# The value projection of a hybrid attention layer: from four pairs with transposes to one seven-product matrix product with tokens on the partitions

## The chip, the cores and the metric

The kernel runs on one core of one Trainium2 chip. The metric is device time in microseconds (us) of that core, the median of several executions of the same program. The profile that is read here is one more execution, taken with the hardware profiler.

## What is computed

One layer of a hybrid encoder: 1024 tokens, model width 1024, 8 heads of chunked softmax attention (A) and 8 heads of stick-breaking attention (B), then gates, an output projection, a LayerNorm, a SwiGLU feed-forward part and a second LayerNorm. What the change touches is the combined input projection:

```python
h = x @ w_in[l]
qa, ka, va, qb, kb, vb, ga, gb = jnp.split(h, split_pts, axis=-1)
```

Each of qa, ka, va, qb, kb, vb is 1024 tokens by 512 columns (8 heads of 64), all in float32. The attention of a head later multiplies its weights (keys by queries) with its 64 columns of va or vb, and there the tokens (keys) have to lie on the partitions.

## The kernel before, in words

**Precision.** Every float32 operand is split into a high part that the tensor engine takes exactly (fp32r) and a low part, `split` (L109): ScalarE copies the high part, VectorE subtracts it (L110, L111). A product of two operands is three matmuls: high by high, high by low, low by high.

**Pairs by seven products.** The projection works on pairs of 128-column tiles, "left" and "right". A pair with the two halves of the tokens is a two by two block product, done with seven products in place of eight, in the order 1, 2, 6, 5, 7, 3, 4 (`pair_steps`, L185, `product`, L168). Each product is 4 steps over the contraction, 3 matmuls each, so 12 matmuls of 128x128 stationary weights with 512 tokens moving; a pair has 84. The sums of x that these products need are made once at the start (`s_sums`, L300, `s13_split`, L311), those of the weights for each pair (`prep_left`, L129; `right_sums_b`, L146; `right_sums_a`, L157; `prep_last`, L162). Products share three PSUM banks, sx, sy and sz; after a product ScalarE copies a bank into the result tile `c` (L199, L208, L212, L420) or VectorE adds it there (L195).

**The list of work** (L232 to L240) has 17 pairs: a query with its key tile (kind qk, 8 of them), two value tiles (kind v, 4 of them), five pairs of gate tiles (kind g). The order is qk, qk, v, qk, qk, v, ... then the gates. The first (qk) is done plainly, in 96 matmuls (`project_plain`, L338). The names in the profile carry the number in this list: wlp5h is the high part of the left weights of pair 5, wap and wbp are right sums, wc the right column of product 3. Pairs 2, 5, 8 and 11 are values.

**The value pair.** Results come out with columns on the partitions. So `out_v` (L393) transposes each of the two tiles in 8 tensor-engine transposes of 128x128 (L401, tile `vtp`), splits them in 8 pieces of 128x256 and stores two heads of 512 KB with rows of 4 KB (L408, `v_dr`). In attention `load_v` (L572) reads one head of 512 KB back in rows of 4 KB (L576).

**What sets the order.** `run_pairs` (L433) calls the products of a pair one after the other and, between them, the loads and sums of later pairs: after the first product the right weights of the next pair, after the second the left weights of the pair after that. Buffers have tags with a fixed number of slots (L44): `gt` (3) and `kp` (4) for raw weights and their sums, `op` (8) for split weights, the tags qs, kh, kl, v with two slots each (`QKV`, taken in turn) for results. A buffer is handed out when its former content has been read for the last time. The framework schedules: each engine's order is fixed at compile time from a model of when operands and slots are ready, with the order of the code as priority, so that an instruction that is ready can be put ahead of one that comes earlier in the code. At run time each engine, and SP's queue which issues all DMAs, goes strictly in the order so fixed. At the start the first two products of three pairs are put ahead (`first=3`), and `rest_of_start` (L541) then makes what the later products lack.

Of the kernel before, what the change touches and what calls it, by code (L numbers as in the profile page):

```python
# [11 lines left out]
F32 = mybir.dt.float32  # L12
F32R = mybir.dt.float32r
AF = mybir.ActivationFunctionType
ALU = mybir.AluOpType
# [3 lines left out]
P = 128  # L19
# [3 lines left out]
DH = 64  # L23
# [7 lines left out]
HW = 512  # L31
LO, HI = slice(0, HW), slice(HW, 2 * HW)
# [13 lines left out]


@with_exitstack
def hybrid_trunk_kernel(ctx: ExitStack, tc, x, xt, w_first, w_in, b_gate, rel_bias, w_proj,
                        w_out, ln1_g, ln1_b, w_ffn_in, w_ffn_out, ln2_g, ln2_b, out):  # L50


# [3 lines left out]
    nc = tc.nc  # L56
# [3 lines left out]
    dr = ctx.enter_context(tc.tile_pool(name="dr", bufs=1, space=DRAM))  # L60
# [3 lines left out]
    def slot(tag, name, dtype=F32):  # L64
        return pool.tile([P, 1024], dtype, tag=tag, name=name, bufs=SLOTS[tag])
# [15 lines left out]

    mm = nc.tensor.matmul
    tr = nc.tensor.transpose
    dma = nc.sync.dma_start


    ident = cst.tile([P, P], F32, name="ident")
# [5 lines left out]

    q_dr = [dr.tile([2 * P, S], F32, name=f"q_dr{i}") for i in range(8)]
    k_dr = [dr.tile([2 * P, S], F32, name=f"k_dr{i}") for i in range(8)]
    v_dr = dram("v_dr", 16)
    y_dr = dram("y_dr", 8)
    g_dr = dram("g_dr", 16)
    m_dr = dram("m_dr", 8)
# [9 lines left out]
    def split(dst_h, dst_l, src):  # L109
        return (nc.scalar.copy(dst_h, src),  # L110
                nc.vector.tensor_tensor(dst_l, src, dst_h.bitcast(F32), ALU.subtract))  # L111
# [45 lines left out]
    def right_sums_a(W, nm, tag):  # L157
        R, ta = W["R"], W["ta"]
        nc.vector.tensor_tensor(ta[:, HI], R[:, HI], R[:, LO], ALU.subtract)
        W["ha"] = split_w(ta, f"wa{nm}", tag)  # L160
# [71 lines left out]
    work = []  # L232
    for br in range(2):
        for i in range(4):
            work.append(("qk", br * 4 + i, br * 12 + i, br * 12 + 4 + i))
            if i % 2:
                work.append(("v", br * 4 + i - 1, br * 12 + 8 + i - 1, br * 12 + 8 + i))

    N_GATE, N_SQUASHED = 5, 4
    work += [("g", j, 24 + j, 32 + j) for j in range(N_GATE)]  # L240
    Wa = [dict() for _ in work]
# [4 lines left out]
    def right(i):  # L246
        prep_right(Wa[i], f"p{i}", w_in[work[i][3]], "op")
        prep_last(Wa[i], f"p{i}", "kp")
# [123 lines left out]
    def project(i):  # L372
        kind, pair = work[i][:2]
        tl = {}

        def tile_of(side):
            if side not in tl:
                tl[side] = cycle(("qs", "kl") if i < 3 and side == "1" else QKV, f"c{side}_{i}")
            return tl[side]

        def c(name):
            return tile_of(name[1])[:, (LO, HI)[int(name[0]) - 1]]

        def out_qk(side):
            scale = (-0.125 if pair < 4 else 0.125) if side == "1" else 1.0
            t = tl[side]
            h = cycle(QKV, f"hi{side}_{i}", F32R)
            nc.scalar.activation(h, t, AF.Copy, scale=scale)
            nc.vector.scalar_tensor_tensor(t, t, scale, h.bitcast(F32), ALU.mult, ALU.subtract)
            d = (q_dr, k_dr)[side == "2"]  # L390
            store_hl(d[pair], h, t)

        def out_v(side):  # L393
            pr = pair + int(side) - 1
            vs = [cycle(QKV, f"v{pr}_{h}", F32R).rearrange("p (t c) -> p t c", t=8)
                  for h in range(2)]
            for hf in range(2):
                tp = bank("tr", f"vtp{pr}_{hf}")
                for j in range(4):
                    o = hf * HW + j * P  # L400
                    tr(tp[:, j * P:(j + 1) * P], tl[side][:, o:o + P], ident)  # L401
                t3 = tp.rearrange("p (t c) -> p t c", t=4)
                ts_ = slice(4 * hf, 4 * hf + 4)
                for h in range(2):
                    split(vs[h][:, ts_, 0:DH], vs[h][:, ts_, DH:P],
                          t3[:, :, h * DH:(h + 1) * DH])
            for h in range(2):
                dma(v_dr[2 * pr + h].rearrange("p (t c) -> p t c", t=8), vs[h].bitcast(F32))  # L408

        def out_g(side):  # L410
            col = (int(side) - 1) * 8 + pair
            if pair < N_SQUASHED:
                nc.scalar.activation(tl[side], tl[side], AF.Sigmoid, bias=bg[:, col:col + 1])
            dma(g_dr[2 * pair + int(side) - 1], tl[side])

        out = dict(qk=out_qk, v=out_v, g=out_g)[kind]

        def done(name, acc):
            if name == "21":
                nc.scalar.copy(c("21"), acc)  # L420
                out("1")
            elif name == "12":
                out("2")

        return pair_steps(f"p{i}", Wa[i], ops_x, c, done, "pv" if i == 3 else "mm")

    def aside_work(i):
        if i == 2:
            small_inputs()
        if i >= len(work) - 9:  # L430
            store_proj(i - len(work) + 9)

    def run_pairs(steps, left, right, also=lambda i: None, first=2, aside=lambda i: None,  # L433
                  then=lambda: None):

        n = len(steps)
        for j in range(first):
            steps[j][0]()
            steps[j][1]()
        then()  # L440
        for i in range(n):
            rest = steps[i][2:] if i < first else steps[i]
            for j, p in enumerate(rest):
                p()
                if j == 0 and i + 1 < n:
                    right(i + 1)
                if j == 1 and i + 2 < n:
                    left(i + 2)
                aside(i)
            also(i)  # L450
# [88 lines left out]
    s_sums(3)  # L539

    def rest_of_start():  # L541
        for kt in range(4):
            s13_split(kt, LO, HI)
        right_sums_a(Wa[1], "p1", "op")
        for kt in range(4):
            s13_split(kt, HI, LO)
        prep_last(Wa[1], "p1", "kp")

    run_pairs([project(i) for i in range(1, len(work))],
              lambda i: left(i + 1) if i > 2 else left_again(3) if i == 2 else None,  # L550
              lambda i: right(i + 1), first=3, then=rest_of_start, also=aside_work)
    first_gate = 2 * N_GATE
    first_w = begin_gate(first_gate, nc.vector)()

# [17 lines left out]
    def load_v(hd):  # L572

        n = 2 * hd["i"] + hd["h"]
        t = slot("v", f"v{n}", F32R)
        dma(t.bitcast(F32), v_dr[n])  # L576
        hd["v"] = t.rearrange("p (t c) -> p t c", t=8)

    def scores(name, hd, b, c0, n):
        q = hd["qs"][:, b * P:(b + 1) * P]  # L580
# [351 lines left out]
    for n, c in enumerate((6, 7, 5, 4, 0, 1, 2, 3)):  # L932
        if n % 2 == 0:
            w = next_w
# [10 lines left out]
        for hf, cs in enumerate((LO, HI)):  # L945
            acc = bank("sc", f"yBps{c}_{hf}")
# [189 lines left out]
    for half_k in range(2):  # L1136
# [136 lines left out]
    first = load_plain(0, 2, ("bw", "bw", "kp", "kp", "bw", "bw", "bw", "kp"))  # L1273
# [34 lines left out]
def layout(inputs):  # L1308

    arr = {n: np.asarray(a)[0] for n, a in inputs.items()}  # L1310
    x = arr["x"][::-1]
    w_in = granules(arr["w_in"])
    w_first = np.stack([w_in[n].reshape(P, 4, 2 * P) for n in (0, 4)], axis=2)
    x_halves = x.T.reshape(KT, P, 2, HW).transpose(2, 0, 1, 3)
    arrs = dict(
        x=x, xt=x_halves,
        w_first=w_first.transpose(1, 0, 2, 3).reshape(4, P, HW), w_in=w_in, b_gate=arr["b_gate"].reshape(16, P).T,
        rel_bias=arr["rel_bias"],
        w_proj=granules(np.concatenate([arr["w_proj_a"], arr["w_proj_b"]])),
        w_out=arr["w_out"], ln1_g=arr["ln1_g"], ln1_b=arr["ln1_b"],  # L1320
        w_ffn_in=granules(arr["w_ffn_in"]), w_ffn_out=arr["w_ffn_out"],
        ln2_g=arr["ln2_g"], ln2_b=arr["ln2_b"])
    return {n: np.ascontiguousarray(a) for n, a in arrs.items()}
# [14 lines left out]
```

## Time and profile before

| | us |
|---|---|
| median of 3 executions | 1439.76 (1439.72 to 1440.11) |
| the profiled execution, its own time | 1440.54 |
| its span in the profile | 1438.8 |
| TensorE busy | 1425.8 |
| VectorE busy | 1030.5 |
| ScalarE busy | 679.0 |
| GpSimd busy | 267.9 |
| the 64 transposes of values, first and last start | 77.7, 249.0 |

The span leaves out what lies around the program's first and last instruction, 1.7 us here. A busy time counts an instruction from its start to its modelled end; matmuls overlap, so their durations add up to more than the time in which they follow one another. The pitch, from one start to the next, has to be taken from windows or from start times. PE is the tensor engine's matmuls and PEld its loads of stationary operands; ACT is ScalarE, DVE VectorE, POOL GpSimd, and SPq the queue of the engine that issues DMAs. In rows of operations the line is that of the code, L180 being the matmul in `product`.

### The profile page before, as it was taken

How to read it: one execution, taken by the hardware profiler on the slowest of the kernel's cores; microseconds unless marked ns; L12 is line 12 of the kernel's file. 1: busy time of each engine (PE TensorE's matmuls, PEld its weight loads, DVE VectorE, ACT ScalarE, POOL GpSimd, SP SyncE). 2: the span in 40 equal slices, each digit the busy share in tenths (PEclk: the TensorE clock that was granted, in tenths of full speed). 3: DMA queues.
4: the chain of work that ended last, by engine and by line, in shares of the span. 5: the costliest groups of instructions: out<-in, count | busy, mean ns of one | idle time of the engine just before them, and what ended most of it. 6: DMA issues, size and time to landing. Idle time of an engine off the chain costs nothing.

```text
span 1438.8 us, 19267 instructions
## 1 busy us (share of the span) xinstructions
PE 1425.8 (99%) x6760; PEld 1182.0 (82%) x6760; DVE 1030.5 (72%) x1664; ACT 679.0 (47%) x1193; POOL 267.9 (19%) x317
## 2 busy tenths in 40 slices
PE   9999999999999999999999999999999999999997
PEld 7788888888888888888888888888888888888886
DVE  8875665544777878877858957667676755978757
ACT  6444444544888788774312734444444433221201
POOL 0000000001555878850014000000000000100016
PEclk9999999999999999999999999999999999999999
DMA  7555657749777487958512223444444457786602
GB/s 249 154 184 176 173 173 224 279 179 248 203 217 198 146 246 249 269 186 287 167 45 88 69 93 132 146 143 151 161 161 150 153 195 263 289 310 234 205 15 103
DMA packets 87921, 262.95 MB, mean 183 GB/s; under 512 B 11008, under 2 KB 11008, under 8 KB 87824
## 3 DMA queue, kind: packets, MB, share of 16 engines
q1 hardware_dynamic: 87824, 261.72, 55.7%
q8 instruction: 53, 0.87, 0.3%
q14 instruction: 44, 0.36, 0.1%
HBM read 169.89 MB, written 88.11 MB: 179 GB/s over the span
## 4 chain that ended last, share of the span: by engine, by line
PE 90%; DVE 4%; ACT 2%; DMA 1%; issue 1%; SPq 1%; POOL 1%; POOLq 0%; DVEq 0%; ACTq 0%
PE sxf L180 16%; PE sxp L180 10%; PE szf L180 8%; PE dx L1264 6%; PE szp L180 5%; PE gps L495 4%; PE syf L180 4%; PE dz L1264 3%; PE yAps L784 3%; PE syp L180 2%; PE tp_b L695 2%; PE tp_a L695 2%; PE ops L117 2%; PE ops L118 2%; PE ops L120 2%; PE dy L1264 2%
## 5 line engine op out<-in xcount | busy, mean ns | idle before, releaser
L1220 POOL TENSOR_TENSOR wdyt<-wdyt 128x512 f32<-128x512 f32 x8 | 11.2, 1394 | 512.3 <-ACT h L1092 422.6
L672 POOL TENSOR_TENSOR w_b<-w_b,kp_b 128x511 f32<-128x511 f32 (+3 forms) x96 | 96.1, 1013 | 33.1 <-DVE kp_b L667 24.0
L667 DVE TENSOR_TENSOR_SCAN kp_b<-kp_b,ident_ps 128x512 f32<-128x512 f32 (+2 forms) x64 | 56.6, 885 | 23.3 <-ACT kp_b L664 22.5
L664 ACT ACTIVATE kp_b<-sc_b 128x512 f32<-128x512 f32 (+3 forms) x96 | 48.4, 504 | 30.7 <-PE sc_b L584 25.8
L972 POOL TENSOR_TENSOR mv<-mv,neghalf 128x1 f32<-128x1 f32 x16 | 23.9, 1493 | 207.7 <-DVE mv L971 207.6
L195 DVE TENSOR_TENSOR c<-sxp,c 128x512 f32<-128x512 f32 x16 | 11.0, 690 | 71.7 <-PE sxp L180 42.8
L607 POOL MEMSET bias<- 64x64 f32 x2 | 0.3, 144 | 323.2 <-ACT bias L603 323.2
L180 PE MATMUL szf<-x1S63h,wcf 128*128 128x512 f32 x168 | 55.1, 389 | 0.0
L111 DVE TENSOR_TENSOR pt_b<-tp_b,pt_b 128x512 fp32r<-128x512 f32 (+1 forms) x96 | 50.0, 544 | 6.8 <-ACT pt_b L110 6.2
L637 POOL TENSOR_SCALAR w_a<-w_a,st_a 128x640 f32<-128x640 f32 (+2 forms) x64 | 42.5, 668 | 62.6 <-PE sc_a L584 25.4
L1195 DVE TENSOR_TENSOR x<-dx,x 128x512 f32<-128x512 f32 x64 | 43.4, 685 | 14.8 <-PE dx L1264 14.8
L111 DVE TENSOR_TENSOR sl<-h,sl 128x512 fp32r<-128x512 f32 x56 | 38.4, 685 | 19.5 <-ACT sl L110 19.5
L110 ACT CAST pt_b<-tp_b 128x512 fp32r<-128x512 f32 (+1 forms) x96 | 47.5, 505 | 8.0 <-PE tp_b L695 7.6
L110 ACT CAST sl<-h 128x512 fp32r<-128x512 f32 x56 | 34.7, 619 | 33.8 <-PE syf L180 17.1
L118 PE MATMUL ops<-wl_o,mh 128*128 128x512 f32 x128 | 50.1, 392 | 0.0
L120 PE MATMUL ops<-wh_o,ml 128*128 128x512 f32 x128 | 49.9, 390 | 0.0
L117 PE MATMUL ops<-wh_o,mh 128*128 128x512 f32 x128 | 49.7, 391 | 0.0
L632 ACT ACTIVATE w_a<-w_a,st_a 128x640 f32<-128x640 f32 (+2 forms) x64 | 44.7, 699 | 10.4 <-DVE st_a L626 8.1
L111 DVE TENSOR_TENSOR pt_a<-tp_a,pt_a 128x512 fp32r<-128x512 f32 (+1 forms) x96 | 44.8, 485 | 6.1 <-ACT pt_a L110 4.7
L665 ACT ACTIVATE w_b<-sc_b 128x511 f32<-128x511 f32 (+3 forms) x96 | 48.5, 506 | 0.0
L1092 ACT ACTIVATE h<-sxf 128x512 f32<-128x512 f32 x21 | 12.6, 598 | 75.8 <-PE sxf L180 75.8
L695 PE MATMUL tp_b<-ident,w_b 128*128 128x128 f32 x288 | 47.8, 273 | 0.4 <-DVE pt_b L111 0.3
(1882 smaller groups left out, 4830.8 us busy)
## 6 DMA issues: line engine op xcount, KB each, us to landing
s_dr<-sl SPq DMA_DIRECT2D x112, 256.0 KB, 2.3
sd<-s_dr SPq DMA_DIRECT2D x56, 512.0 KB, 4.8
wLf<-in_w_ffn_in_dram SPq DMA_DIRECT2D x22, 512.0 KB, 4.4
wRf<-in_w_ffn_in_dram SPq DMA_DIRECT2D x22, 512.0 KB, 3.6
wLp<-in_w_in_dram SPq DMA_DIRECT2D x17, 512.0 KB, 5.6
wRp<-in_w_in_dram SPq DMA_DIRECT2D x16, 512.0 KB, 5.6
v_dr<-v SPq DMA_DIRECT2D x16, 512.0 KB, 4.0
v<-v_dr SPq DMA_DIRECT2D x16, 512.0 KB, 4.6
```

The source lines that it names most:

```text
L110: return (nc.scalar.copy(dst_h, src), nc.vector.tensor_tensor(dst_l, src, dst_h.bitcast(F32), ALU.subtract))
L111: nc.vector.tensor_tensor(dst_l, src, dst_h.bitcast(F32), ALU.subtract))
L117: mm(acc, lh, rh, start=(i == 0), stop=False)
L118: mm(acc, lh, rl, start=False, stop=False)
L120: mm(acc, ll, rh, start=False, stop=(i == n))
L180: mm(acc, lw[:, ks], rx, start=(first and kt == i == 0), stop=(kt == 3 and i == 2), skip_group_check=not first)
L495: mm(acc[hf], lw[:, ks], rx[k][:, (LO, HI)[hf]], start=(k == j == 0), stop=(k == KT - 1 and j == 2))
L665: nc.scalar.activation(be[:, m0:e], sc[:, m0 - c0:n], AF.Sigmoid)
L667: nc.vector.tensor_tensor_scan(kp[:, 0:e], kp[:, 0:e], ident_ps()[:, 0:e], 0.0, ALU.mult, ALU.add)
L672: nc.gpsimd.tensor_tensor(be[:, m0:e], be[:, m0:e], kp[:, m0 - 1:e - 1], ALU.mult)
L695: tr(tp[:, (qb - lo_q) * P:(qb - lo_q + 1) * P], wt[qb - q0][:, (kb - qb) * P:(kb - qb + 1) * P], ident)
L1264: mm(acc, a, b, start=(first and i == n == 0), stop=(i == n - 1 == 1), skip_group_check=not first)
```

## The change

The four value pairs leave the list of work. In their place stands one piece of work at position 5, after qk4 (list then: qk0 to qk4, values, qk5 to qk7, five gates; 14 entries). It takes the whole value projection, 1024 tokens by 1024 contraction by 1024 columns (512 of A, 512 of B), as one two by two block product by seven. Now 128 tokens of the sums of x are the stationary operand and 512 columns of weights move, so the results have tokens on the partitions and there are no transposes. Each of the seven products is 2 halves of the contraction by 4 token tiles by 2 steps by 3 matmuls, 48 in all.

`v_load` loads three of the four weight blocks (each two tiles of 512 KB) into `gt` and `kp` slots. `v_prepare(p)` makes the split weights of product p, two tiles at a time (4 `op` slots of the 8), and is called at the start of the product before it. For product 6 it loads the fourth block into two `QKV` slots and makes three subtractions of 128x1024 per half; for product 7 it loads that block again into `gt` and subtracts once. Results sit in four banks each of two groups (tr, tr, tr, pv; and mm, mm, sc, sc), and every bank is copied or added to a result tile in pieces of 128x512, then split and stored in rows of 4 KB. In DRAM the values are now two tensors, one for each branch, with a row of 32 KB for a partition; attention reads a head's 512 KB from there in pieces of 512 bytes.

Around it, the loads of pair 6 (qk5) and the left weights of qk6 are called after products 3 and 4 of the values, where they were otherwise called during the pairs before. `aside_work` (the projection weights split ahead) follows the shorter list. At the start, `right_sums_a` of pair 1 is called ahead of the low halves of the x sums.

```diff
-    v_dr = dram("v_dr", 16)
+    v_dr = [dr.tile([P, 8192], F32, name=f"v_dr{i}") for i in range(2)]
...
             work.append(("qk", br * 4 + i, br * 12 + i, br * 12 + 4 + i))
-            if i % 2:
-                work.append(("v", br * 4 + i - 1, br * 12 + 8 + i - 1, br * 12 + 8 + i))
+    V_AT = 5
+    work.insert(V_AT, ("v",))
...
-        def out_v(side):
-            pr = pair + int(side) - 1
-            vs = [cycle(QKV, f"v{pr}_{h}", F32R).rearrange("p (t c) -> p t c", t=8)
-                  for h in range(2)]
-            for hf in range(2):
-                tp = bank("tr", f"vtp{pr}_{hf}")
-                for j in range(4):
-                    o = hf * HW + j * P
-                    tr(tp[:, j * P:(j + 1) * P], tl[side][:, o:o + P], ident)
-                t3 = tp.rearrange("p (t c) -> p t c", t=4)
-                ts_ = slice(4 * hf, 4 * hf + 4)
-                for h in range(2):
-                    split(vs[h][:, ts_, 0:DH], vs[h][:, ts_, DH:P],
-                          t3[:, :, h * DH:(h + 1) * DH])
-            for h in range(2):
-                dma(v_dr[2 * pr + h].rearrange("p (t c) -> p t c", t=8), vs[h].bitcast(F32))
...
+    def v_load():
+        for n, (blk, tags) in enumerate(((0, ("gt", "gt")), (3, ("gt", "kp")), (2, ("kp", "kp")))):
+            for h, tag in enumerate(tags):
+                v_src[n][h] = slot(tag, f"wv{blk}_{h}")
+        for n, blk in ((0, 0), (2, 2), (1, 3)):
+            for h in range(2):
+                dma(v_src[n][h], w_v[blk, h])
+
+    def v_prepare(p):
+        put, sub = nc.vector.tensor_tensor, ALU.subtract
+        v_ops[p] = []
+        for h in range(2):
+            X, U, Z = (v_src[n][h] for n in range(3))
+            hi, lo = (slot("op", f"v{s}{p}_{h}", F32R) for s in "hl")
+            src = {1: X, 2: Z, 5: X, 3: U, 4: Z}.get(p)
+            if src is None:
+                src = cycle(QKV, f"wv1_{p}{h}") if p == 6 else slot("gt", f"wv1_{p}{h}")
+                dma(src, w_v[1, h])
+                if p == 6:
+                    put(X, src, X, sub)
+                    put(src, U, X, sub)
+                    put(Z, Z, src, sub)
+                else:
+                    put(src, U, src, sub)
+            split(hi, lo, src)
+            v_ops[p].append((hi, lo))
...
+        def step(p, following):
+            accs = by if p in (2, 5, 3) else bx
+            first = p in (1, 2, 5)
+            def run():
+                if following:
+                    v_prepare(following)
+                if first:
+                    for j in range(4):
+                        tag = ("mm", "mm", "sc", "sc")[j] if accs is by else ("tr", "tr", "tr", "pv")[j]
+                        accs[j] = bank(tag, f"v{p}_{j}")
+                for h in range(2):
+                    for j in range(4):
+                        for i in range(2):
+                            kt = 2 * h + i
+                            xh_, xl_ = (x[:, j * P:(j + 1) * P] for x in ops_x[p][kt])
+                            wh, wl = (w[:, (LO, HI)[i]] for w in v_ops[p][h])
+                            for n, (a, b) in enumerate(((xh_, wh), (xh_, wl), (xl_, wh))):
+                                mm(accs[j], a, b, start=(first and kt == n == 0),
+                                   stop=(kt == 3 and n == 2), skip_group_check=True)
+                for j in range(4):
+                    acc = spread(accs[j])
+                    if p == 4:
+                        done("21", j, acc)
+                        continue
+                    name = {1: "11", 2: "11", 6: "12", 3: "12", 5: "22", 7: "22"}[p]
+                    raw = tile_of(name, j)[1]
+                    if p in (1, 6, 5):
+                        nc.scalar.copy(raw, acc)
+                    else:
+                        nc.vector.tensor_tensor(raw, acc, raw, ALU.add)
+                        done(name, j, raw)
+            return run
...
             for j, p in enumerate(rest):
                 p()
+                if i == wide:
+                    if j == 5:
+                        left(i + 1)
+                    if j == 6:
+                        right(i + 1)
+                        left(i + 2)
+                    continue
                 if j == 0 and i + 1 < n:
                     right(i + 1)
-                if j == 1 and i + 2 < n:
+                if j == 1 and i + 2 < n and wide not in (i + 1, i + 2):
                     left(i + 2)
...
     def rest_of_start():
+        right_sums_a(Wa[1], "p1", "op")
         for kt in range(4):
             s13_split(kt, LO, HI)
-        right_sums_a(Wa[1], "p1", "op")
...
-        dma(t.bitcast(F32), v_dr[n])
         hd["v"] = t.rearrange("p (t c) -> p t c", t=8)
+        src = v_dr[n // 8].rearrange("p (t n c) -> p n t c", t=8, n=8)
+        dma(hd["v"].bitcast(F32), src[:, n % 8])
```

Here `done` (in `v_steps`) splits a result piece into the high and low columns of its tile and stores 128 tokens by 512 columns, and `spread` views a bank as 8 heads of 64 columns.

More of the change, by code (lines that the diff above doesn't have):

```diff
@@ L48, in hybrid_trunk_kernel @@
 @with_exitstack
-def hybrid_trunk_kernel(ctx: ExitStack, tc, x, xt, w_first, w_in, b_gate, rel_bias, w_proj,
+def hybrid_trunk_kernel(ctx: ExitStack, tc, x, xt, w_first, w_v, w_in, b_gate, rel_bias, w_proj,
                         w_out, ln1_g, ln1_b, w_ffn_in, w_ffn_out, ln2_g, ln2_b, out):
@@ L414, in out_g @@
             dma(g_dr[2 * pair + int(side) - 1], tl[side])
-        out = dict(qk=out_qk, v=out_v, g=out_g)[kind]
+        out = dict(qk=out_qk, g=out_g)[kind]
         def done(name, acc):
@@ L425, in project @@
         return pair_steps(f"p{i}", Wa[i], ops_x, c, done, "pv" if i == 3 else "mm")
+    v_src = [[None] * 2 for _ in range(3)]
+    v_ops = {}
+    def v_load():
[23 more added lines that the diff above has]
+            v_ops[p].append((hi, lo))
@@ new lines, in v_steps, with spread, tile_of, done @@
+    def v_steps():
+        bx, by, tiles = [None] * 4, [None] * 4, {}
+        def spread(ap):
+            return ap.rearrange("p (n c) -> p n c", n=8)
+        def tile_of(name, j):
+            if (name, j) not in tiles:
+                tiles[name, j] = cycle(QKV, f"vc{name}_{j}")
+            o = spread(tiles[name, j])
+            return o[:, :, 0:DH].bitcast(F32R), o[:, :, DH:P]
+        def done(name, j, src):
+            hi, lo = tile_of(name, j)
+            split(hi, lo, src)
+            br, t = int(name in ("12", "22")), j + 4 * int(name[0] == "2")
+            dma(v_dr[br][:, t * 1024:(t + 1) * 1024], tiles[name, j])
+        def step(p, following):
[30 more added lines that the diff above has]
+            return run
+        order = (1, 2, 6, 5, 7, 3, 4)
+        return [step(p, q) for p, q in zip(order, order[1:] + (None,))]
@@ L433, in run_pairs @@
     def run_pairs(steps, left, right, also=lambda i: None, first=2, aside=lambda i: None,
-                  then=lambda: None):
+                  then=lambda: None, wide=None):
         n = len(steps)
@@ L547, in rest_of_start, with right_or_v @@
         prep_last(Wa[1], "p1", "kp")
-    run_pairs([project(i) for i in range(1, len(work))],
+    def right_or_v(i):
+        if i + 1 == V_AT:
+            v_load()
+            v_prepare(1)
+        else:
+            right(i + 1)
+    run_pairs([v_steps() if i == V_AT else project(i) for i in range(1, len(work))],
               lambda i: left(i + 1) if i > 2 else left_again(3) if i == 2 else None,
-              lambda i: right(i + 1), first=3, then=rest_of_start, also=aside_work)
+              right_or_v, first=3, then=rest_of_start, also=aside_work, wide=V_AT - 1)
     first_gate = 2 * N_GATE
@@ L1313, in layout @@
     w_first = np.stack([w_in[n].reshape(P, 4, 2 * P) for n in (0, 4)], axis=2)
+    w_v = np.stack([arr["w_in"][:, c:c + HW] for c in (1024, 2560)], axis=1)
+    w_v = w_v.reshape(2, 2, 2, P, 2, HW).transpose(0, 4, 1, 3, 2, 5).reshape(4, 2, P, 1024)
     x_halves = x.T.reshape(KT, P, 2, HW).transpose(2, 0, 1, 3)
@@ L1316, in layout @@
         x=x, xt=x_halves,
-        w_first=w_first.transpose(1, 0, 2, 3).reshape(4, P, HW), w_in=w_in, b_gate=arr["b_gate"].reshape(16, P).T,
+        w_first=w_first.transpose(1, 0, 2, 3).reshape(4, P, HW), w_v=w_v, w_in=w_in,
+        b_gate=arr["b_gate"].reshape(16, P).T,
         rel_bias=arr["rel_bias"],
```

## The prediction

> **What bounds the kernel now.** I read the page's busy times first, then the waits of the tensor engine, then windows cut at the starts of the pairs.
>
> ```profile
> PE 1425.8 (99%) x6760; PEld 1182.0 (82%) x6760; DVE 1030.5 (72%) x1664; ACT 679.0 (47%) x1193; POOL 267.9 (19%) x317
> PEclk9999999999999999999999999999999999999999
> ...
> PE szp L180 <- ACT wap1h L110: 0.6, 1, 0.6
> ...
> PE vtp L401 <- DVE c L195: 0.4, 1, 0.4
> ```
>
> TensorE is never without work for long, at full granted clock: its waits for other engines are fractions of a us. So work taken from TensorE comes off the span, and work added to another engine costs nothing until it makes TensorE wait.
>
> ```profile
> 28.06:89.60 61.54, 60.45 (x269) 48.36 (x268) 52.34 (x77) 31.60 (x50) 0.00 (x0) 1.00 0.54 168
> 89.60:108.64 19.04, 19.04 (x85) 15.77 (x84) 12.35 (x16) 8.16 (x11) 0.00 (x0) 1.00 0.53 167
> 108.64:148.69 40.05, 40.05 (x186) 32.99 (x184) 22.89 (x33) 16.99 (x27) 0.00 (x0) 1.00 0.52 158
> ...
> 167.73:207.78 40.05, 40.05 (x185) 32.99 (x184) 24.18 (x34) 18.11 (x28) 0.00 (x0) 1.00 0.57 184
> 226.82:266.92 40.10, 40.10 (x185) 32.99 (x184) 25.52 (x37) 20.24 (x31) 0.00 (x0) 1.00 0.78 257
> ```
>
> The columns are window, length, then busy time and number on PE, PEld, DVE, ACT, POOL, granted clock, DMA share, GB/s. The second window is pair 4, a query and key pair alone: 84 loads of a stationary operand in 19.04 us, a pitch of 0.2267 us. The next three hold a value pair and a query pair each: 184 loads, 168 of them for products, 16 for transposes.
>
> **The change part by part.**
>
> *The transposes go.* Two pairs without transposes take 2 x 19.04 = 38.08 us. The windows take 40.05, 40.05 and 40.10, so the 16 transposes cost 1.97, 1.97 and 2.02 us, 0.12 us each. The first value pair lies in the first window: 252 matmuls at 0.2267 are 57.12 of its 61.54 us; 4.42 are left, of which I give 1.97 to the transposes and 0.4 to the wait of vtp above. Together 1.97 + 1.97 + 2.02 + 1.97 + 0.4 = **8.3 us off**.
>
> ```profile
> L401 PE MATMUL vtp<-ident,c x64: 270/273/329, 77.7 to 249.1; 128*128 128x128 f32 x64
> ...
> 126.39 1.09 PE L401 MATMUL vtp<-ident,c 128*128 128x128 f32 x8
> 127.24 0.48 PE L180 MATMUL sxp<-xh,wbp5h 128*128 128x512 f32 x1
> ```
>
> One transpose is listed with 273 ns, but eight of them and the switch to the next matmul take 127.24 - 126.39 = 0.85 us. Their listed durations overlap, so 64 x 0.273 = 17.5 us is no saving; the windows are. "TensorE: Matmul & The Clock Gate" of the Trainium skill, Part 4, gives a transpose about 275 ns in a kernel's context; as a duration the trace agrees (273 ns), as a price per transpose it does not (0.12 us).
>
> *The matmuls stay.* Four value pairs are 4 x 84 = 336 matmuls, the new product 7 x 48 = 336, again 128x128 stationary and 512 moving. What moves is now the weights. The trace has that form in the last stage, where sums of activations are stationary:
>
> ```profile
> 1230.00:1330.00 100.00, 100.00 (x443) 82.68 (x442) 85.92 (x119) 22.13 (x25) 8.42 (x6) 1.00 0.82 289
> ```
>
> 442 in 100 us is 0.226 each. So **0 us** here; a product of 48 takes 10.88 us, the seven 76.2.
>
> *VectorE and ScalarE in the new stage.*
>
> ```profile
> L389 DVE SCALAR_TENSOR_TENSOR c<-c,hi 128x1024 f32<-128x1024 f32 x14 | 17.1, 1222 | 0.7 <-ACT hi L388 0.7
> L111 DVE TENSOR_TENSOR v<-vtp,v 128x256 fp32r<-128x256 f32 x32 | 12.9, 420 | 2.6 <-ACT v L110 2.4
> ...
> L195 DVE TENSOR_TENSOR c<-sxp,c 128x512 f32<-128x512 f32 x15 | 10.4, 690 | 65.1 <-PE sxp L180 36.3 <-issue 24.0 <-ACT wh_proj L462 4.8
> ...
> L199 ACT COPY c<-sxp 128x512 f32<-128x512 f32 x16 | 9.3, 589 | 3.9 <-PE sxp L180 3.7 <-DVE xraw L308 0.2
> ...
> L110 ACT CAST wlp7h<-wLp x1: 1053/1053/1053, 128.7 to 128.7; 128x1024 fp32r<-128x1024 f32 x1
> L111 DVE TENSOR_TENSOR wlp7l<-wLp,wlp7h x1: 1227/1227/1227, 129.8 to 129.8; 128x1024 fp32r<-128x1024 f32 x1
> ```
>
> Added on VectorE: 14 splits and 8 subtractions of 128x1024 (1.23 us) and 12 additions and 16 splits of 128x512 (0.69): 27.1 + 19.3 = 46 us of 76, 61%. Taken away per value pair: four sums, three additions and a short split (0.69 each), three long splits, eight pieces of 0.42: 5.5 + 3.7 + 3.4 = 12.6, four times 50 us. ScalarE: 14 x 1.05 + 28 x 0.59 = 31 us of 76. Both are covered by the matmuls; what matters is whether each product's weights are in time.
>
> *In time or not.* With 8 `op` slots, 4 per product, the weights of the next product can be split from the moment the product before the present one is done, half by half, with 10.88 us to do 2 x (1.05 + 1.23) = 4.6 us. Banks: a product waits for a bank that was written two products earlier. Only product 6 is different: its fourth block has to be loaded into `QKV` slots, the first of which by their order is that of qk4's left result, free when the last store of q has landed.
>
> ```profile
> 114.00 1.17 SPq L336 DMA_DIRECT2D q_dr<-c  x1
> 115.21 1.10 SPq L142 DMA_DIRECT2D wRp<-in_w_in_dram  x1
> 116.36 1.08 SPq L131 DMA_DIRECT2D wLp<-in_w_in_dram  x1
> 127.56 0.33 SPq L142 DMA_DIRECT2D wRp<-in_w_in_dram  x1
> 128.38 4.63 SPq L408 DMA_DIRECT2D v_dr<-v  x4
> ...
> DMA to landing us min/median/max: 3.2/4.2/7.4
> ...
> DMA to landing us min/median/max: 3.9/5.6/7.0
> ```
>
> (Landings: first row q_dr, second wLp.) In pair 4, which ended at 108.64, that store was issued 5.4 us after the end. Landing 4.2, load 5.6, three subtractions 3.7, cast 1.05, low part 1.23: 21.2 us after the values begin. Product 6 begins after 2 x 10.88 = 21.8. In time by 0.6 at the medians; with the longest landings (7.4 and 7.0) 4.0 late; with the shortest, early. If late, product 6 waits and nothing of later products can stand in, as they need the same sums. Behind the waiting load on SP's queue stand only the stores of product 2's results; behind the waiting subtraction on VectorE stand product 2's additions, whose banks are wanted again by product 5, another 10.9 us later. I take **+0.5**, nearest to the medians (ends 0 and 4.0).
>
> *After the values.* Pair 6's loads are called behind products 3 and 4. If they were issued there, they would come late (below). But the queue goes by readiness: at 127.56 a right load is issued ahead of pair 5's four value stores at 128.38, although the code calls its next right load only after pair 6's first product. The `gt` slots are free about when products 7 and 3 start, `op` slots from product 3 on. So I cost it at 0.
>
> *One right sum sooner.*
>
> ```profile
> 46.88 0.39 PE L180 MATMUL sxp<-s24h,wbp1l 128*128 128x512 f32 x1
> 47.84 0.50 PE L180 MATMUL szp<-s13h,wap1h 128*128 128x512 f32 x1 [0.57 <-ACT wap1h L110]
> ...
> 49.10 0.50 PE L180 MATMUL szp<-s13h,wap1l 128*128 128x512 f32 x1
> ...
> 64.07 1.23 DVE L111 TENSOR_TENSOR wbp3l<-tbp,wbp3h 128x1024 fp32r<-128x1024 f32 x1 [0.52 <-ACT wbp3h L110]
> ```
>
> From 46.88 to 49.10 five matmuls start (the rows left out hold three), 2.22 us for 1.13: 1.1 us are lost to wap1. Made sooner, they are regained here. But VectorE is busy for 52.34 of the first window's 61.54 us, the sum only changes places with others, and wbp3l is finished at 65.3 either way, so part of it turns into a wait for wbp3. Between 0 and 1.1 off; I take **0.5**, the middle.
>
> *DMA.* Values now load 10 blocks of 512 KB where 8 were loaded, with a DMA share of 0.5 to 0.8 in the windows: hidden. In attention a head's values come as 1024 pieces of 512 bytes.
>
> ```profile
> q1 hardware_dynamic: 87824, 261.72, 55.7%
> ...
> 327.00:484.00 157.00, 155.65 (x910) 131.71 (x909) 112.81 (x385) 116.95 (x292) 81.37 (x104) 1.00 0.76 206
> 484.00:652.00 168.00, 167.34 (x940) 141.46 (x939) 137.70 (x198) 129.91 (x302) 123.88 (x168) 1.00 0.72 221
> ...
> 414.01 0.33 SPq L576 DMA_DIRECT2D v<-v_dr  x1
> ...
> 429.63 0.32 SPq L576 DMA_DIRECT2D v<-v_dr  x1
> ```
>
> 55.7% of 16 x 1438.8 us over 87,824 packets is 146 ns for a mean packet of 2980 bytes. By bytes a 512-byte packet is 25 ns, at most it is 146. A load then takes 1.6 to 9.3 us of the 16 engines, against 1.6 now. Heads follow one another by 15.6 us and a head's slot is refilled one head ahead, so a landing some us later is hidden. I take 0, nearer to the bytes. "DMA: Bandwidth & Descriptors" of the Trainium skill speaks mildly against the pieces: "Why small descriptors are slow" adds about 3 cycles per packet to one per 32 bytes, an estimated 19% at 512 bytes, which would still be hidden; no run here shows it yet.
>
> **Sum.** -8.3 - 0.5 + 0.5 = -8.3. Span 1438.8 to 1430.5; the profiled execution's own time 1440.54 to 1432.2; the median shown, 1439.76, is 0.78 below that execution, so **1431.5 us**.
>
> **Rivals.**
>
> *Weights late inside the values.* Product 6 waits the full 4.0 us, or a later product some: 1431.5 + 3.5 = 1435. For it: the margin of 0.6. Against: the landings would all have to be long.
>
> *A gap behind the values: no change.* If pair 6's weights are fetched where the code calls them, the right weights leave after the last splits (about 2 us), land 5.6 later, take three sums (2.1) and a split (2.3): 12 us, of which its first two products cover 5.4: 6.6 us of waiting (the left weights, 2 + 5.6 + 2.3 = 9.9 us after product 3, are covered by product 4's 10.9): 1438.1. Against it: the queue's order by readiness.
>
> *Small pieces fill the DMA engines: slower.* Place: attention, 16 value loads. At 146 ns a packet each load adds 7.7 us of all 16 engines per 15.6 us: share 0.76 + 0.49 = 1.25, so 8 heads of A lengthen by 0.25 x 15.6 = 3.9 us each, and those of B, with 168 / 8 = 21 us, go to 0.72 + 0.37 = 1.09, some 1.9 us more each: +46, about 1478. It decides once the share passes 1, from 3.8 us more per load, a packet of 84 ns. For it: small packets may cost as much as large. Against it: nothing in the trace shows it.
>
> *The transposes cost their listed durations.* 64 x 0.273 = 17.5 off: 1422. The Trainium skill's transpose price would give the same. Against: the windows.
>
> **How the numbers follow.** Forecast (1429.4 to 1433) 0.70; weights late in the values (1433 to 1437) 0.11; gap behind them (1437 to 1442.6) 0.09; DMA filled (above) 0.07; transposes dearer (below 1429) 0.03. The low end takes the full 1.1 for the sum, no wait at product 6, and the 1.0 us of other waits that the first window still has (4.42 - 1.97 - 0.4 - 1.1). The range **1429 to 1437** holds 0.81. This kernel's time can be told from no change from about 0.2%, 2.9 us: faster 0.83, same 0.09, slower 0.08.
>
> **What would show it.** Right: no vtp rows; seven products of about 10.9 us with a pitch of 0.227 and no wait at their starts; pair 6 following at once; heads in attention as far apart as before, value loads landing below 10 us. Wrong: a wait of TensorE for a low or high part of product 6's weights or of pair 6's; a DMA share near 1 and later starts of heads in attention; wap1's wait gone but one for wbp3 grown by as much means that the moved sum gave nothing.

## The result: slower by 0.24%

The changed kernel takes 1443.40 us (median of 14 runs, 1442.29 to 1444.73), the kernel before 1440.11 us on the same chip (14 runs). The ratio is 1.0024, with a 95% interval of 1.0015 to 1.0032. The forecast was 1431.5 us, in a range of 1429 to 1437: the time lies outside it, on the other side of the kernel before.

**The profile after.** The profiled execution took 1444.35 us, its span is 1442.6. From its page, the busy line and the granted clock, and from the list of TensorE's waits (in all, times, longest):

```profile
PE 1421.1 (99%) x6696; PEld 1178.6 (82%) x6696; DVE 1028.6 (71%) x1638; ACT 673.0 (47%) x1171; POOL 267.8 (19%) x317
PEclk9998999999999999999999999999999999999999
```

```profile
PE v L479 <- ACT vh L110: 9.3, 1, 9.3
```

The 64 transposes are gone (6760 matmuls, now 6696). In their place stands one wait of 9.3 us for `vh`, the high part of a value weight, and in the same place the granted clock shows its only 8. Windows cut at the stages (same columns as before: length, PE, PEld, DVE, ACT, POOL, granted clock, DMA share, GB/s) say what each is worth:

```profile
28.06:86.59 58.53, 57.90 (x254) 47.23 (x253) 47.77 (x65) 29.29 (x42) 0.00 (x0) 1.00 0.50 146
86.59:115.18 28.59, 28.59 (x125) 22.95 (x124) 10.77 (x12) 9.32 (x12) 0.00 (x0) 1.00 0.68 199
115.18:194.66 79.48, 70.20 (x297) 57.30 (x297) 50.72 (x60) 31.34 (x44) 0.00 (x0) 0.94 0.51 171
194.66:213.70 19.04, 19.04 (x85) 15.77 (x84) 10.23 (x14) 8.03 (x11) 0.00 (x0) 1.00 0.52 187
```

The start is 3.01 us shorter (58.53 for 61.54), and the three later value pairs' transposes, 1.97 + 1.97 + 2.02 = 5.96 us, are saved as well: 8.97 off. The two windows in the middle are qk4 and the values: 108.07 us for 84 + 336 matmuls, which at 0.2267 take 95.21: 12.86 on. The sum, +3.89, is the span's difference, 1442.6 - 1438.8 = 3.8. So one stage holds the whole answer. Pair 6 follows at once, in 19.04 us.

**Where the 12.86 us lie.** Product 6 and what stands ahead of it, in three windows:

```profile
115.02:127.94 12.92, 12.92 (x58) 10.51 (x56) 5.51 (x7) 5.14 (x8) 0.00 (x0) 1.00 0.78 202
127.94:137.38 9.44, 0.16 (x1) 0.00 (x1) 9.15 (x10) 1.89 (x4) 0.00 (x0) 0.77 0.76 261
137.38:151.14 13.76, 13.76 (x48) 10.91 (x49) 8.26 (x8) 5.63 (x8) 0.00 (x0) 0.79 0.31 97
```

qk4's last matmul has been issued at 115.02. Then 57 matmuls of products 1 and 2 run at full pitch, 12.92 us. Then TensorE rests 9.44 us while VectorE is busy for 9.15 of them. Then the 48 matmuls of product 6 take 13.76 us, 2.88 more than 10.88. Rest and slow matmuls make 12.3; some 0.5 more goes where qk4's matmuls and those of product 1 alternate.

The prediction gave product 6 a cover of 21.8 us, two products of 48 matmuls. The cover is 12.92 us because the scheduler had put 39 of product 1's 48 matmuls among qk4's products, where qk4 would otherwise have waited for its copies (experiment 3 shows these waits):

```profile
99.78 4.99 PE v L479 x22
104.76 2.85 PE sxp L180 x12
107.61 0.91 PE v L479 x4
108.52 2.82 PE sxp L180 x12
111.34 0.91 PE v L479 x4
112.24 2.94 PE sxp L180 x12
115.18 10.21 PE v L479 x45
...
126.73 2.90 DMA v_dr<-vc
...
130.12 1.23 DVE wv L434
...
135.03 1.24 DVE wv L435
...
136.28 1.05 ACT vh L110
...
137.38 7.80 PE v L479 x21
```

This is the chain of waits (start, length, what). Above, `v` stands between the `sxp` of qk4. Below, the profile leads the chain to product 6 through the store of product 2's first result, the subtractions and the cast. VectorE's own rows show that the store is not what held the subtractions:

```profile
124.06 0.69 DVE L491 TENSOR_TENSOR vc<-v,vc 128x512 f32<-128x512 f32 x1 [4.92 <-PE v L479]
...
128.74 1.46 DVE L111 TENSOR_TENSOR vc<-vc 128x512 f32<-128x512 f32 x2
130.12 1.22 DVE L434 TENSOR_TENSOR wv<-wv,wv 128x1024 f32<-128x1024 f32 x1
...
133.77 1.22 DVE L434 TENSOR_TENSOR wv<-wv,wv 128x1024 f32<-128x1024 f32 x1
```

From 124.06 to 130.20 VectorE adds and splits product 2's results as TensorE finishes them, and the subtractions follow without a gap. So in this kernel the order on VectorE came last: work that needs product 2's matmuls stands ahead of the subtractions for product 6. How late the loads are as well, SP's queue shows:

```profile
120.31 0.62 SPq L336 DMA_DIRECT2D q_dr<-c  x1
121.04 1.01 SPq L432 DMA_DIRECT2D wv<-in_w_v_dram  x1
126.73 0.33 SPq L459 DMA_DIRECT2D v_dr<-vc  x1
127.18 0.37 SPq L432 DMA_DIRECT2D wv<-in_w_v_dram  x1
```

The two halves of the fourth weight block are loaded at 121.04 and 127.18, the first right behind qk4's last store, the second (which product 6 uses first) behind a store of product 2's first result, which waits for the matmuls of the cover itself. The second half landed 4.9 us after its issue, at 132.1, so it was there 1.7 us ahead of its first subtraction at 133.77. From qk4's end at 115.02 to product 6 at 137.38 it is 22.4 us. The prediction had worked out 21.2.

### The profile page after: what moved, and what is told of

Its sections match the earlier page's. It is cut to its first block, busy times and chain, and to the rows that moved or that the text cites. A ratio compares the mean times of both kernels' runs of the same rounds, so it can differ in the third digit from the quotient of the medians.

```text
span 1442.6 us, 19078 instructions
## 1 busy us (share of the span) xinstructions
PE 1421.1 (99%) x6696; PEld 1178.6 (82%) x6696; DVE 1028.6 (71%) x1638; ACT 673.0 (47%) x1171; POOL 267.8 (19%) x317
## 4 chain that ended last, share of the span: by engine, by line
PE 93%; DVE 3%; ACT 1%; DMA 1%; issue 1%; POOL 0%; SPq 0%; POOLq 0%; DVEq 0%; ACTq 0%
PE sxf L180 16%; PE sxp L180 8%; PE szf L180 8%; PE dx L1350 6%; PE v L479 5%; PE gps L573 4%; PE szp L180 4%; PE syf L180 4%; PE dz L1350 3%; PE yAps L870 3%; PE syp L180 2%; PE tp_b L781 2%; PE tp_a L781 2%; PE ops L118 2%; PE ops L117 2%; PE ops L120 2%
## 5 line engine op out<-in xcount | busy, mean ns | idle before, releaser
L753 DVE TENSOR_TENSOR_SCAN kp_b<-kp_b,ident_ps 128x512 f32<-128x512 f32 (+2 forms) x64 | 56.6, 885 | 23.3 <-ACT kp_b L750 22.4
L110 ACT CAST pt_a<-tp_a 128x512 fp32r<-128x512 f32 (+1 forms) x96 | 39.1, 432 | 11.0 <-PE tp_a L781 10.7
```

The source lines that it names most:

```text
L110: return (nc.scalar.copy(dst_h, src), nc.vector.tensor_tensor(dst_l, src, dst_h.bitcast(F32), ALU.subtract))
L753: nc.vector.tensor_tensor_scan(kp[:, 0:e], kp[:, 0:e], ident_ps()[:, 0:e], 0.0, ALU.mult, ALU.add)
```

## The experiments

**Theory.** The fourth block's load waits for qk4's stores, 22.4 us of chain then stand against 12.9 us of cover, and TensorE rests; the slow clock is a consequence of the rest. **Rivals.** The order of VectorE and the queue alone sets the end (product 2's additions ahead of the subtractions); the hoisted matmuls alone do; the slow matmuls have a cause of their own; small DMA pieces cost time elsewhere.

| kernel | us | ratio to before (95%) | waits ahead of and in product 6 | its 48 matmuls |
|---|---|---|---|---|
| changed kernel | 1443.40 | 1.0024 (1.0015 to 1.0032) | 9.3 | 13.76 |
| fourth block early | 1431.98 | 0.9944 (0.9931 to 0.9956) | none | 10.88 |
| subtractions first | 1440.18 | 1.0000 (0.9991 to 1.0008) | 5.2 | 13.14 |
| product 1 kept | 1437.72 | 0.9985 (0.9976 to 0.9994) | 1.24 and 1.13 | 12.47 |
| both orders kept | 1433.49 | 0.9956 (0.9944 to 0.9969) | none | 10.88 |
| rest filled | 1441.55 | 1.0009 (1.0001 to 1.0018) | 1.13 | 11.42 |
| early, sum put back | 1432.02 | 0.9945 (0.9931 to 0.9958) | none | 10.88 |
| before, sum alone | 1441.06 | 1.0006 (0.9997 to 1.0014) | | |
| before, small pieces | 1440.29 | 1.0003 (0.9994 to 1.0012) | | |

**1. The fourth block early.** Its two buffers are taken, and its loads called, with those of the other three.

```diff
+    v_fourth = []
     def v_load():
...
+        for h in range(2):
+            v_fourth.append(cycle(QKV, f"wv1_6{h}"))
+            dma(v_fourth[h], w_v[1, h])
...
-                src = cycle(QKV, f"wv1_{p}{h}") if p == 6 else slot("gt", f"wv1_{p}{h}")
-                dma(src, w_v[1, h])
+                src = v_fourth[h] if p == 6 else slot("gt", f"wv1_{p}{h}")
+                if p != 6:
+                    dma(src, w_v[1, h])
```

> The fourth weight block that product 6 needs is given its two buffers and loaded together with the other three, before qk4's last products, and nothing else is edited. In the changed kernel TensorE waits 9.3 us ahead of product 6 and its 48 matmuls then take 13.76 instead of 10.88 us. Theory (the block is loaded late, because its buffers come free only with qk4's stores): both vanish, 9.3 + 2.9 = 12.2 us off, about 1431 us, some 9 below the kernel before. If the early load only moves the wait (the block now holds two result buffers that qk4's results want, so qk4 waits for them): a wait of some us in qk4, 1436 to 1443. If something of the product form itself costs the time (weights as moving operand, pieces of 512 bytes): 1440 or more, with no wait to be seen.

Measured 1431.98. In its trace the loads leave at 103.81, ahead of qk4's stores, TensorE waits for nothing in qk4 or the values, and windows from qk4's end and over product 6 read:

```profile
114.52:127.44 12.92, 12.92 (x59) 10.70 (x57) 11.12 (x11) 6.92 (x10) 0.00 (x0) 1.00 0.62 149
127.44:138.32 10.88, 10.88 (x50) 9.01 (x48) 7.49 (x10) 5.24 (x8) 0.00 (x0) 1.00 0.69 251
```

The 57 matmuls of cover are the same as in the changed kernel, the 48 of product 6 follow at once and at full clock. The product form, moving weights and pieces of 512 bytes, costs nothing that shows: this kernel is faster than both, by 0.56% than the kernel before. The early load also moves the subtractions ahead, so it does not tell load and order apart.

**2. The subtractions first.** Only orders change; buffers and loads stay.

```diff
-                        nc.vector.tensor_tensor(raw, acc, raw, ALU.add)
+                        add = nc.vector.tensor_tensor(raw, acc, raw, ALU.add)
+                        if p == 2:
+                            tc.keep_in_program_order(add)
```

> Buffers and loads as in the changed kernel; VectorE's additions of product 2's results are kept behind the subtractions for product 6, and with that both loads of the fourth block stand ahead of product 2's stores in SP's queue. Rival theory (the order on VectorE and in the queue is what comes last, the buffers came free early enough): the wait of 9.3 us goes down to 2 or less, 1433 to 1435 us. Main theory (the buffers come free with qk4's stores, 22 us of work stand behind that point and only 12.9 us of matmuls are left to cover it): the second half's load leaves 5.5 us sooner, the wait goes from 9.3 to about 5 or 6, and the time to 1437 to 1440.

The kernel took 1440.18 us, with a wait of 5.2 us ahead of product 6. These are a wait in SP's queue, the second load, the first subtraction on VectorE, and the chain:

```profile
SPq L432 <- DMA q_dr<-c: 2.1, 1, 2.1
```

```profile
124.09 0.33 SPq L432 DMA_DIRECT2D wv<-in_w_v_dram  x1
```

```profile
126.11 1.23 DVE L434 TENSOR_TENSOR wv<-wv,wv 128x1024 f32<-128x1024 f32 x1 [7.11 <-DMA wv<-in_w_v_dram]
```

```profile
120.90 5.19 DMA wv<-in_w_v_dram
...
126.11 1.24 DVE wv L434
...
130.90 1.15 DVE wv L435
...
132.07 1.05 ACT vh L110
...
133.17 6.95 PE v L479 x20
```

With nothing of product 2 ahead, the second load waits 2.1 us for qk4's store to land and leaves at 124.09, 3.1 us sooner than in the changed kernel. VectorE now idles 7.1 us for the first half, so here the load comes last. The chain from qk4's end is 133.17 - 114.88 = 18.3 us, still 5 above the cover of 12.92. Order on VectorE and in the queue is worth 4 of the 22.4 us; the rival that it is everything falls. The time came out just above the 1437 to 1440 expected, as the slow matmuls lost 2.26 us and not in proportion to the rest.

**3. Product 1 kept in its place.**

```diff
-                                mm(accs[j], a, b, start=(first and kt == n == 0),
-                                   stop=(kt == 3 and n == 2), skip_group_check=True)
+                                ins = mm(accs[j], a, b, start=(first and kt == n == 0),
+                                         stop=(kt == 3 and n == 2), skip_group_check=True)
+                                if p == 1 and h == j == i == n == 0:
+                                    tc.keep_in_program_order(ins)
```

> The first matmul of the values' product 1 is kept at its place in the order of the code, so that 12 of its 48 matmuls, in place of 39, run ahead of qk4's end. Nothing else is edited; the order on VectorE follows. Theory of the lost cover (the matmuls put into qk4's gaps are missing later, between qk4's stores and product 6): qk4 ends 5 or 6 us sooner, the wait ahead of product 6 falls from 9.3 to about 3 us, the time to 1434 to 1437. If the hoisting did no harm (qk4 would only have waited itself): the wait comes back inside qk4, and the time stays at 1442 to 1444.

The kernel took 1437.72 us, a little above the range of the theory of the lost cover. qk4 ends at 110.67, not 115.02, and now waits itself (0.68 and 0.78 us and slower changes); 84 matmuls stand behind it and the rest is 1.24 us. VectorE's order shifted too (only one of product 2's four additions, at 125.89, still stands ahead of the second half's subtractions), so the shares of order and cover are not pure here.

**4. Both orders kept**, the edits of 2 and 3 together.

> The changed kernel with both orders kept (product 1's first matmul in its place, product 2's additions behind the subtractions), the buffers and loads of the fourth block as in the changed kernel. Main theory, by its sum: from qk4's end to product 6 the chain took 18.3 us with the subtractions first, and products 1 and 2 leave 84 matmuls x 0.227 = 19.0 us behind qk4's end. So no wait at product 6, or under 0.5 us, and no slow matmuls after it; what remains against the early load are 2 us of waits within qk4. 1434 to 1435 us, against 1437.7 with product 1 alone kept and 1440.2 with the subtractions alone. If the buffers themselves are too few whatever the order: 1437 or more.

The kernel took 1433.49 us, half a us below the range expected. These are TensorE's waits from 85 to 200 us, all of them in qk4, and the windows of qk4 and of the values:

```profile
PE sxp L180 <- DVE c L195: 0.8, 1, 0.8
PE sxp L180 <- ACT c L208: 0.7, 1, 0.7
```

```profile
86.04:110.12 24.08, 22.62 (x98) 17.71 (x96) 10.77 (x12) 8.38 (x11) 0.00 (x0) 1.00 0.78 228
110.12:183.56 73.44, 73.44 (x326) 60.81 (x324) 50.37 (x60) 32.41 (x46) 0.00 (x0) 1.00 0.57 186
```

The test by arithmetic holds: the 18.3 us of chain of experiment 2 against 84 x 0.2267 = 19.04 us of cover leave no rest, and 324 matmuls run at 0.2267 throughout. Here the load is as late, against qk4's end, as in experiment 2; what experiment 2 lacked was cover. So the wait of 9.3 us had two causes: 4.1 of it go with the order alone, and the 5.2 that are left go when the cover is back as well. In qk4 2.3 us are lost here (24.08 for 96 x 0.2267 = 21.76) where the changed kernel lost some 0.5, so the hoisting had saved 1.8: it was no loss in itself, it spent ahead what was needed later.

**5. The rest filled.** In product 6, ahead of its own:

```diff
+                if p == 6:
+                    u, w = ops_x[2][0][0], ops_x[2][1][0]
+                    for n in range(36):
+                        tc.keep_in_program_order(mm(accs[n % 4], u[:, 0:P], w, start=False,
+                                                    stop=False, skip_group_check=True))
```

> 36 matmuls of two tiles of x are put between products 2 and 6, on the accumulators of product 6, so its result is changed; 36 x 0.227 = 8.2 us of the wait of 9.3 are filled, and what product 6 waits for is untouched. If the slow matmuls of product 6 (13.76 for 10.88 us, granted clock 0.62 to 0.76) follow from TensorE's rest: product 6 begins at the same time and takes 10.9 us, 1440.5 us in all. If they wait for late low parts or for the weights' port: 13.76 stays, 1443.4. If the clock falls with the work done and not with the rest: longer than 1443.4.

The kernel took 1441.55 us. These are windows over the 36 added matmuls, the rest that is left, and product 6:

```profile
127.13:135.45 8.32, 8.32 (x37) 6.57 (x35) 8.06 (x9) 0.81 (x2) 0.00 (x0) 1.00 0.86 296
135.45:136.58 1.13, 0.00 (x1) 0.00 (x0) 1.10 (x1) 1.10 (x2) 0.00 (x0) 1.00 0.00 0
136.58:142.00 5.42, 5.29 (x22) 4.09 (x23) 4.67 (x5) 2.80 (x3) 0.00 (x0) 1.00 0.14 40
142.00:148.00 6.00, 6.00 (x28) 4.96 (x27) 3.31 (x3) 2.63 (x5) 0.00 (x0) 1.00 0.40 141
```

From qk4's end to product 6 it is 22.37 us as before (136.58 - 114.21; 22.36 in the changed kernel), and yet the kernel is faster by 1.85 us, and its span by 2.9, with 36 matmuls more. The clock stays at 1.00 and product 6 takes 11.42 us. So 2.3 of the 2.88 us follow from the rest, through the clock; about 0.5 stays at the start of product 6 even so, where its fifth matmul, the first that needs a low part of a weight, starts 1.32 us after the first (137.90 - 136.58) in place of 0.91. The median lies 1.0 above the 1440.5 expected. Of this 0.5 is this remainder; the other half stays open, but the profiled execution of the changed kernel, from which the expectation was made, was itself 0.95 above its median.

**6. The sum alone, and the early kernel without it.** In the kernel before, `right_sums_a` is called ahead of the low halves; in that of experiment 1 it is put back.

```diff
+        right_sums_a(Wa[1], "p1", "op")
         for kt in range(4):
             s13_split(kt, LO, HI)
-        right_sums_a(Wa[1], "p1", "op")
```

> The kernel before with one edit: the right sum of pair 1 is called ahead of the low halves of the x sums. The prediction gave it 0.5 us (0 to 1.1), because five matmuls there start in 2.22 us for 1.13. If the sum is only early enough for wap1: 0.5 to 1.1 off. If the sums just change places and wbp3, which ended at 65.3, is late by as much: 0, with wap1's wait gone and one for a later sum grown by as much. Both are near what can be told from no change by the times; the end of pairs 1 to 3 in the trace (89.60 before) tells them apart.

> The kernel with the fourth block loaded early (1431.98 us), with the right sum of pair 1 put back behind the low halves. With no value pair in the start, pairs 1 to 3 ended at 86.27 there. If the moved sum gives in this surrounding what was foreseen (0 to 1.1): 1432 to 1433. If the start's sums bind each other: 1432, the end of pair 3 unchanged. If the moved sum makes the waits for wbp3 and wap3: a little faster than 1432.

They took 1441.06 us (no difference from the kernel before that can be told) and 1432.02 beside 1431.98. These are TensorE's waits from 28 to 112 us in the first:

```profile
PE sxp L180 <- ACT c L208: 0.9, 1, 0.9
PE sxp L180 <- ACT wbp3h L110: 0.4, 1, 0.4
PE szp L180 <- ACT wap3h L110: 0.2, 1, 0.2
```

wap1's wait is gone; waits for wbp3 and wap3 of 0.6 us in all stand in its place, and one of 0.9 for a copy is new there. Pair 3 ends 0.39 us sooner (89.21) in the first; in the second, without the sum, 0.38 later (86.65) than with it. The traces give the sum 0.4 us, the times nothing.

**7. Small pieces in the kernel before**, both ways.

```diff
-    v_dr = dram("v_dr", 16)
+    v_dr = [dr.tile([P, 8192], F32, name=f"v_dr{i}") for i in range(2)]
+
+    def v_of(n):
+        return v_dr[n // 8].rearrange("p (t n c) -> p n t c", t=8, n=8)[:, n % 8]
...
-                dma(v_dr[2 * pr + h].rearrange("p (t c) -> p t c", t=8), vs[h].bitcast(F32))
+                dma(v_of(2 * pr + h), vs[h].bitcast(F32))
...
-        dma(t.bitcast(F32), v_dr[n])
+        dma(hd["v"].bitcast(F32), v_of(n))
```

> The kernel before with one edit: values lie in DRAM in rows of 32 KB, so each head of 512 KB is both stored and read back in 1024 pieces of 512 bytes (the changed kernel reads so, and stores in rows of 4 KB). No other edit. If small pieces cost by their bytes, or are hidden as the changed kernel's attention says (its heads lie as far apart as before): 1439 to 1441.5, the DMA's busy share as before. If a packet costs its mean of 146 ns whatever its size: each load and each store adds some 7.7 us of all 16 DMA engines, 1460 to 1490.

The kernel took 1440.29 us. This is the row of the big queue (packets, MB, share):

```profile
q1 hardware_dynamic: 116496, 261.72, 56.7%
```

28,672 packets more than before, and the share goes from 55.7 to 56.7%: 0.567 x 16 x 1438.5 - 0.557 x 16 x 1438.8 = some 230 us over all engines, 8 ns for each added packet (the shares are rounded, so 7 to 9). The rival of full DMA engines asked for 146 ns.

## Why the prediction was wrong, point by point

- **Transposes, -8.3.** Right. The three later pairs gave 5.96 as read from the windows, and the start 3.01 where 1.97 + 0.4 for the transposes and 0.5 for the sum had been put. Experiment 1, in which nothing else goes wrong, has a span of 1430.3; the prediction's sum was 1430.5. The rival of 17.5 us by listed durations is refuted.
- **Matmuls stay, 0.** Right: 324 at 0.2267 in experiment 4.
- **Wait at product 6, +0.5.** This is the step that failed, by two of its premises. The first is the cover: "Product 6 begins after 2 x 10.88 = 21.8" assumed that all of products 1 and 2 lie behind qk4's end. The schedule had put 39 matmuls, 8.8 us, ahead of it, and 12.92 us were left. The text had drawn on the framework's readiness order to cost the loads behind the values at 0, and did not apply the same rule to the matmuls of product 1, which were ready during qk4.
- **"Behind the waiting subtraction on VectorE stand product 2's additions".** This is the second premise, and it was the other way round: the additions and their splits stood ahead of the subtractions (124.06 to 130.12), and a store of product 2's first result stood ahead of the second load. Experiment 2 puts order and queue together at 4 us. In experiment 4, with this order as the prediction had it and 84 of the 96 matmuls of products 1 and 2 behind qk4's end, product 6 does not wait, and the time, 1433.49, lies in the range of the forecast. The longest lateness that the prediction allowed was 4.0; the rest came to 9.4.
- **The chain of 21.2 us.** It lies near the measured 22.4 by luck. The links that the prediction added up, with the order that it assumed, took 18.3 us in experiment 2; the 4 us more in the changed kernel are the order, which it had not put in.
- **A wait costs its length.** Also wrong, and not said: after 9.3 us of rest product 6 took 2.88 us more, and experiment 5 puts 2.3 of them on the slow clock. The rival "weights late" carried 3.5 us at most and no such term.
- **After the values, 0; small pieces, 0.** Right: pair 6 follows in 19.04 us, and experiment 7 tells no difference. TensorE waits once for a value load in attention, 0.2 us. Attention, in windows of the changed kernel of the same lengths as before and 4 us later, issues as many matmuls (912 and 940 where there were 910 and 940), at the same DMA share:

```profile
331.00:488.00 157.00, 155.68 (x912) 132.02 (x911) 113.35 (x386) 117.03 (x292) 81.65 (x104) 1.00 0.76 207
488.00:656.00 168.00, 167.39 (x940) 141.49 (x939) 137.89 (x198) 129.73 (x302) 123.52 (x168) 1.00 0.73 221
```

- **One right sum, -0.5.** Near: 0.4 in the traces, not to be told in the times.

With 9.44 + 2.88 + 0.5 = 12.8 in place of the 0.5 for product 6, the prediction's terms give -8.3 - 0.5 + 12.8 = +4.0; the spans differ by 3.8.

## What to carry to other kernels

When a load must meet a deadline, count its cover from the static order of the engine, not from the order of the code: work that is ready early is used up early, in somebody else's gaps, and is missing behind the point at which the load can start. Ask of each block which earlier result's buffer it takes, and load it before that result exists, or order the work so that cover follows the release. Look as well at the engine that prepares the operand: work there that needs the cover's own results, and stands ahead of the preparing, cannot be hidden behind that cover. A rest of TensorE can cost more than its length: here rests of 5.2 and 9.3 us were followed by products that took 2.3 and 2.9 us longer.

## What the runs showed of the hardware

After rests of 5.2 and 9.3 us TensorE's matmuls start at about half pace and return to full pace some us later. This is product 6 in the changed kernel:

```profile
137.38 1.65 PE L479 MATMUL v<-vh,s24h 128*128 128x512 f32 x3 [9.28 <-ACT vh L110]
...
141.43 0.63 PE L479 MATMUL v<-vh,s24l 128*128 128x512 f32 x1
141.85 0.63 PE L479 MATMUL v<-vh,s24h 128*128 128x512 f32 x1
...
143.43 0.40 PE L479 MATMUL v<-vh,s24l 128*128 128x512 f32 x1
143.66 0.39 PE L479 MATMUL v<-vh,s24h 128*128 128x512 f32 x1
```

The pitch is 0.42 to 0.43 us (141.85 - 141.43), then 0.23 from about 143.2, 5.8 us after the restart. The granted clock shows the same: in windows it is 1.00 from 127.94 to 133.0, the first 5.1 us of the rest, and 0.50 from there to 143.2, 10.2 us in all. In experiment 2 it is 1.00 for the first 3.0 us of the rest of 5.2 us and then 0.50 from 130.8 to 137.6, 6.8 us in all, so it came back about 4.5 us after the restart. After 1.24 us of rest in experiment 3 the clock stayed at 1.00.

The Trainium skill, "TensorE: Matmul & The Clock Gate", Part 1, says that the clock is halved after an idle window of about 3.4 us and comes back after one busy window of that length, the windows running freely, and gives 426.7 ns for 512 columns on the halved clock. These runs agree on the pitch and on which rests halve the clock. The slow stretches of 10.2 and 6.8 us are three and two times 3.4 us, and a busy stretch of 5.8 and 4.5 us before the clock returns fits the end of one window and then a whole one.
